# A transformer trunk on one core: the second part's down projection as four pairs in seven products, the third part's ninth gate/up unit ahead of it

## The chip, the core and the metric

The kernel runs on one core of a Trainium2 chip. The metric is the time of one execution on the device, in microseconds. The kernel before was run three times; its median is what the changed kernel is compared with.

## The reference, cut to what matters

Two layers, each with a feed-forward, a mixer (convolution and differential attention) and a second feed-forward, over 512 positions of 1024 channels in float32. The change lies in the feed-forwards, of which there are four:

```python
D_MODEL, SEQ, DEPTH, D_FF = 1024, 512, 2, 2816

def swiglu(h, w_gate, w_up, w_down):
    return (jax.nn.silu(h @ w_gate) * (h @ w_up)) @ w_down

for l in range(DEPTH):
    x = x + 0.5 * swiglu(rms_norm(x, ffn1_norm[l]), ffn1_w_gate[l], ffn1_w_up[l], ffn1_w_down[l])
    ...  # mixer
    x = x + 0.5 * swiglu(rms_norm(x, ffn2_norm[l]), ffn2_w_gate[l], ffn2_w_up[l], ffn2_w_down[l])
```

## The kernel before

**Number format.** Activations lie with channels on the 128 partitions and positions along the row. Every float32 product is made of three TensorE matmuls in the fp32r format: each operand is split into a high part (ScalarE copies it, `hi`, L364 for weights) and a low part (VectorE subtracts, `lo`, L368 for weights), and high x high, high x low and low x high are added up in PSUM.

**The three parts of a feed-forward.** The 2816 hidden channels are 22 tiles of 128. `PARTS` gives each part as (first tile, number of tiles, pairs): the first has five tiles and is computed plainly, the second eight tiles (5 to 12), the third nine (13 to 21). In the second and third parts the work is cut into units. A gate/up unit (`GateUp`) makes one hidden tile: its gate and its up projection together are a 2 x 2 block product (two outputs, two halves of the input channels, two halves of the positions), done in seven products of 256 columns instead of eight, after Strassen and Winograd. Each product has four steps over the input channels and three matmuls a step, so a unit is 84 matmuls of 256 columns. After the part's gate/up units come four down units (`Down`, q = 0 to 3), each for two output tiles, A = 2q and B = 2q + 1 of x. A down unit takes hidden tiles two by two: a pair of hidden tiles and two output tiles are again a 2 x 2 block, in seven products. Hidden tiles that are in no pair are multiplied plainly, with matmuls of 512 columns (`plain`; into the bank of its own for B, `ps_d`, it is called `spare`).

**What the units need.** For a weight unit, GpSimdE forms four sums of the weight quarters (`sums`, L355 to L358); then ScalarE and VectorE split four chunks A, B, C and D. For a pair of hidden tiles, the first tile is held as it is (`hold`), the second's difference is formed, and `combine` (L664 to L671) makes three sums, split into `hi`, `lo` and `four` (the tiles `hs`): `four` holds high and low part of the fourth sum, whose high part is L669 on ScalarE and whose low part is L671 on VectorE. `hi` and `lo` come from L668 and L670. The seven products name their operands: `t1`, `b11`, `b21`, `b22` read the split hidden tiles (`hh`, `hl`), and `t2`, `t3`, `t4` the sums.

**Order.** `Unit.body` runs one unit: product `t1`, then `t4`, then the rest of the unit before (`prev.rest()`, its product `t3`), then `b11`, `b21`, `b22`, `t2`, and `close`. In between it loads the next unit and splits its chunks in the order A, B, D, C, finishes the hidden tile of the unit before in three steps, and combines the pair of the unit two before. The first matmul of every product is pinned to its place in the program, so TensorE's order is that of `body`; the other engines' instructions are placed by the scheduler, once, when the program is built. Each engine then runs its list in order. The high parts of the 1024-wide chunks have four buffers in turn (`whi`), the raw chunks five (`wraw`), the D chunks one (`wraw2`). The copy L427 (`keep`, of the first bank after `t2`) must be over before `rest` of the same unit may start.

**The end of a feed-forward.** The last down unit (q = 3 of the third part) makes `spare` early, after `t4`; in `close` it makes the plain product for A, adds (L580), writes A into x (L571), subtracts and writes for B (L587, L571), and `rest` adds the last product into B. After each write `after` prepares the tile for the next stage, or, in the last feed-forward, sends it to the output.

Of the kernel before, what the change touches and what calls it, by code (L numbers as in the profile page):

```python
# [11 lines left out]
F32 = mybir.dt.float32  # L12
# [3 lines left out]
ALU = mybir.AluOpType  # L16
AX = mybir.AxisListType

P = 128
DEPTH = 2  # L20
SEQ = 512
DM = 1024
KT = DM // P
# [18 lines left out]
HS = SEQ // 2  # L42


PARTS = ((0, 5, 0), (5, 8, 3), (13, 9, 3))
PLAIN = PARTS[0][1]
PIN = False

# [20 lines left out]
def trunk(ctx: ExitStack, tc: tile.TileContext, xt, par, lamv, relb, onehot,  # L69
# [264 lines left out]
    def pinned(ins, pin=PIN):  # L334
        if pin:
            tc.keep_in_program_order(ins)
        return ins
# [4 lines left out]
    def by_two(t):  # L342
        return t.rearrange("p (n c) -> p n c", n=2)

    class Unit:
# [1 line left out]

        WIDE = {"A": ("", 1024), "B": ("", 1024), "C": ("", 1024), "D": ("2", 512)}

        def __init__(self, fp, turn):  # L350
            self.fp, self.turn = fp, turn
            self.parts, self.raw, self.cols = {}, {}, {}

        def sums(self, u1, u2, g1, g2, d, m0, m1):
# [36 lines left out]
        def body(self, nxt, prev, prev2):  # L391
            if nxt:
                nxt.load()
            self.begin()
            self.go(self.c, "u2u1", "t1", first=True)
            pinned(S.activation(self.keep[:, 3], self.c, AF.Copy))
            if nxt:
                nxt.hi("A")
                nxt.lo("A")
            self.go(self.d, "u2", "t4", first=True)  # L400
            self.early()
            if nxt and self.early_free:
# [24 lines left out]
            pinned(S.activation(self.keep[:, 2], self.a, AF.Copy))  # L427
# [7 lines left out]
        early_free = True  # L435

        def early(self):
            pass
# [4 lines left out]
        def finish(self, n):  # L443
            pass

        def extras(self):
            pass

    class GateUp(Unit):
        steps = KT // 2  # L450

        def __init__(self, fp, turn, halves, g, u, n, gated):
            super().__init__(fp, turn)
# [34 lines left out]
        def finish(self, n):  # L488
            self.gated.add(self.n, self.banks[0], n)

        def extras(self):
            self.gated.combine(self.n, self.banks[0])

    class Down(Unit):
        def __init__(self, fp, turn, dn, m0, many, pairs, q, h, after, last):
            super().__init__(fp, turn)
# [51 lines left out]
        def plain(self, ps, n, first=False):  # L548
            if 2 * self.steps == self.many:
                return  # L550
            w = [
                self.w("BA"[n], k) if k < 8 else self.w(*self.ninth[n])
                for k in range(2 * self.steps, self.many)
            ]
            self.product(ps, zip(w, self.h.hh[2 * self.steps :]), first)

        def spare(self):
            if 2 * self.steps < self.many:
# [41 lines left out]

    class Gated:

        def __init__(self, fp, pairs):
            self.fp, self.pairs = fp, pairs
            self.hh, self.sums, self.held, self.slots = [], [], {}, []

        def part(self):

# [12 lines left out]
        def plain(self, n, us):  # L621
            hi = self.fp.tile([P, SEQ], F32R, tag=f"hh{n}", name="hh")
            lo = self.fp.tile([P, SEQ], F32R, tag=f"hl{n}", name="hl")
            S.activation(hi, us, AF.Copy)
            V.tensor_tensor(lo, us, f32(hi), op=ALU.subtract)
            self.hh.append((hi, lo))

        def paired(self, n):
            return n < 2 * self.pairs
# [1 line left out]
        def add(self, n, us, step):  # L631
            a, b = slice(0, HS), slice(HS, SEQ)
            first = self.paired(n) and n % 2 == 0
            if step == 0:
                if first:
                    self.held[n] = self.fp.tile([P, SEQ], F32, tag=("hh8", "hl8")[n // 2 % 2], name="hold")
                    pinned(S.activation(self.held[n], us, AF.Copy))
                else:
                    self.part_hi(n, us)
            if step == 1:  # L640
                if first:
                    pinned(V.tensor_tensor(us[:, b], self.held[n][:, a], us[:, b], op=ALU.subtract))
                    self.part_hi(n, us)
                else:
                    self.part_lo(us)
            if step == 2 and first:
                self.part_lo(us)

        def part_hi(self, n, us):
            hi = self.fp.tile([P, SEQ], F32R, tag=f"hh{n}", name="hh")  # L650
            lo = self.fp.tile([P, SEQ], F32R, tag=f"hl{n}", name="hl")
            pinned(S.activation(hi, us, AF.Copy))
            self.hh.append((hi, lo))

        def part_lo(self, us):
            hi, lo = self.hh[-1]
            pinned(V.tensor_tensor(lo, us, f32(hi), op=ALU.subtract))

        def combine(self, n, us):
            if not self.paired(n) or n % 2 == 0:  # L660
                return
            a, b = slice(0, HS), slice(HS, SEQ)
            t = self.held[n - 1]
            pinned(V.tensor_tensor(t[:, b], us[:, b], t[:, b], op=ALU.subtract))  # L664
            pinned(V.scalar_tensor_tensor(t[:, a], t[:, a], -1.0, t[:, b], op0=ALU.mult, op1=ALU.subtract))
            pinned(V.scalar_tensor_tensor(us[:, a], us[:, a], -1.0, t[:, a], op0=ALU.mult, op1=ALU.subtract))
# [3 lines left out]
            pinned(V.tensor_tensor(lo, t, f32(hi), op=ALU.subtract))  # L670
            pinned(V.tensor_tensor(four[:, b], us[:, a], f32(four[:, a]), op=ALU.subtract))  # L671
            self.sums.append((hi, lo, four))
# [9 lines left out]
    def ffn(pr, gu, dn, after, turn, lead=None, aside=None):  # L682
        with tc.tile_pool(name="ffn", bufs=1) as fp:
            r = halves = None
            held, h = [], Gated(fp, 0)
            for m in range(PLAIN):
                if m == 4 and aside:
                    aside()
# [44 lines left out]
            units = []  # L733
            for m0, many, pairs in PARTS[1:]:
                h = Gated(fp, pairs)
# [392 lines left out]
    turn = 0  # L1128
# [91 lines left out]
```

## Time and profile before

| | |
|---|---|
| median of three runs | 1781.65 us (1780.59 to 1783.45) |
| profiled execution | 1779.9 us |
| its span | 1778.1 us |
| TensorE busy | 1765.5 us, 99% of the span |
| VectorE, ScalarE, GpSimdE busy | 78%, 56%, 54% |
| granted TensorE clock | 1.000 |

The span runs from the first to the last instruction; the profiled execution's own time is 1.8 us longer. Engines go by the names PE (TensorE's matmuls), PEld (its weight loads), DVE (VectorE), ACT (ScalarE), POOL (GpSimdE) and SP. A row of the timeline gives start in us, duration in us, engine, line, instruction, tiles, shape and count, and in brackets the idle time of the engine before it with what ended it. Matmul rows overlap: the time from start to start is what one costs.

### The profile page before, as it was taken

Reading aid. Unit: us, or ns where it says so; the run is one execution under the profiler, and the core shown is the slowest. Engines: PE = TensorE matmul, PEld = TensorE weight load, DVE = VectorE, ACT = ScalarE, POOL = GpSimd, SP = SyncE. Lnnn points to the kernel's source line nnn. Section 1 sums busy time; section 2 is a strip of 40 time slices with the busy share of each in tenths; the row PEclk is TensorE's granted clock in tenths of the full one; section 3 lists DMA queues with packets and bytes.
Section 4 is the critical chain, followed back from the end, with each engine's and each line's share of the span. In section 5 each row is a group of like instructions: output and inputs, shape, how many; then the busy total and the mean of one; then the engine's idle time right before and its main releaser. Section 6 shows DMA issues by size and latency. Waiting matters only on the chain.

```text
span 1778.1 us, 30234 instructions
## 1 busy us (share of the span) xinstructions
PE 1765.5 (99%) x11725; PEld 1617.3 (91%) x11725; DVE 1394.3 (78%) x1997; ACT 986.9 (56%) x1579; POOL 965.4 (54%) x665
## 2 busy tenths in 40 slices
PE   9999999999999999999999999999999999999999
PEld 7899999988788899999988999999877888999998
DVE  6978787868857978788767887877788588787875
ACT  6456565645844456466534664665558354564663
POOL 2276566379952156566303655653898433565661
PEclk9999999999999999999999999999999999999999
DMA  6233333423122223333332333334230232333332
GB/s 225 96 113 96 107 107 105 144 85 96 47 72 83 83 95 107 107 98 118 118 95 72 108 96 108 106 102 148 72 119 25 72 107 73 106 96 108 107 105 75
DMA packets 74225, 177.87 MB, mean 100 GB/s; under 512 B 8951, under 2 KB 30726, under 8 KB 74080
## 3 DMA queue, kind: packets, MB, share of 16 engines
q1 hardware_dynamic: 72480, 174.10, 31.1%
q8 instruction: 92, 1.51, 0.3%
q0 software_dynamic: 1312, 1.67, 0.3%
q14 instruction: 53, 0.43, 0.1%
q10 hardware_dynamic: 288, 0.16, 0.0%
HBM read 173.79 MB, written 3.42 MB: 100 GB/s over the span
## 4 chain that ended last, share of the span: by engine, by line
PE 89%; DVE 6%; issue 2%; POOL 2%; ACT 1%; DMA 0%; DVEq 0%; SPq 0%; ACTq 0%
PE ps_pair L378 48%; PE ps_pair L141 5%; PE ps_pair L142 5%; PE ps_pair L138 5%; PE ps_d L378 3%; DVE wlo L368 2%; PE ps_d L141 2%; PE ps_d L142 2%; PE ps_d L138 2%; PE ps_sc L990 2%; PE ps_pair L867 2%; PE ps_pair L868 2%; PE ps_pair L866 2%; PE ps_out L138 1%; PE ps_out L142 1%
## 5 line engine op out<-in xcount | busy, mean ns | idle before, releaser
L368 DVE TENSOR_TENSOR wlo<-wraw,whi 128x1024 fp32r<-128x1024 f32 (+4 forms) x400 | 510.3, 1277 | 171.9 <-ACT whi L364 171.4
L364 ACT ACTIVATE whi<-wraw 128x1024 fp32r<-128x1024 f32 (+4 forms) x400 | 373.6, 935 | 333.5 <-PE ps_pair L378 153.1
L355 POOL TENSOR_TENSOR wraw<-wraw 128x512 f32<-128x512 f32 (+1 forms) x100 | 127.8, 1278 | 554.7 <-DVE wlo L368 366.5
L378 PE MATMUL ps_pair<-acth,wlo 128*128 128x256 f32 x1088 | 307.9, 283 | 0.0
L378 PE MATMUL ps_pair<-actl,whi 128*128 128x256 f32 x1088 | 307.9, 283 | 0.0
L378 PE MATMUL ps_pair<-acth,whi 128*128 128x256 f32 x1088 | 307.9, 283 | 0.0
L378 PE MATMUL ps_pair<-th,whi 128*128 128x256 f32 x816 | 231.8, 284 | 1.2 <-ACT keep L427 0.4
L378 PE MATMUL ps_pair<-tl,whi 128*128 128x256 f32 x816 | 230.9, 283 | 0.0
L378 PE MATMUL ps_pair<-th,wlo 128*128 128x256 f32 x816 | 230.9, 283 | 0.0
L378 PEld LDWEIGHTS ps_pair<-actl,whi 128*128 128x128 f32 x1088 | 208.9, 192 | 0.2
L378 PEld LDWEIGHTS ps_pair<-acth,whi 128*128 128x128 f32 x1088 | 208.9, 192 | 0.2
L378 PEld LDWEIGHTS ps_pair<-acth,wlo 128*128 128x128 f32 x1088 | 208.9, 192 | 0.0
L101 ACT ACTIVATE whi<-wraw 128x1024 fp32r<-128x1024 f32 (+3 forms) x124 | 123.2, 1000 | 150.5 <-PE ps_pair L141 84.3
L141 PE MATMUL ps_pair<-actl,whi 128*128 128x512 f32 x448 | 174.6, 390 | 0.6 <-DVE actl L227 0.5
L142 PE MATMUL ps_pair<-acth,wlo 128*128 128x512 f32 x448 | 174.2, 390 | 0.0
L138 PE MATMUL ps_pair<-acth,whi 128*128 128x512 f32 x448 | 173.6, 393 | 0.1
L357 POOL TENSOR_TENSOR wraw<-wraw 128x512 f32<-128x512 f32 (+1 forms) x100 | 169.3, 1693 | 7.9
L358 POOL TENSOR_TENSOR wraw<-wraw 128x512 f32<-128x512 f32 (+1 forms) x100 | 164.3, 1643 | 7.8
L378 PEld LDWEIGHTS ps_pair<-th,whi 128*128 128x128 f32 x816 | 156.6, 192 | 3.1 <-ACT keep L427 3.1
L378 PEld LDWEIGHTS ps_pair<-th,wlo 128*128 128x128 f32 x816 | 156.6, 192 | 0.0
L378 PEld LDWEIGHTS ps_pair<-tl,whi 128*128 128x128 f32 x816 | 156.6, 192 | 0.0
L356 POOL TENSOR_TENSOR wraw<-wraw 128x512 f32<-128x512 f32 (+1 forms) x100 | 149.9, 1499 | 7.6
(203 smaller groups left out, 4402.1 us busy)
## 6 DMA issues: line engine op xcount, KB each, us to landing
wraw<-in_gu SPq DMA_DIRECT2D x172, 512.0 KB, 3.5
wraw<-in_wqkv SPq DMA_DIRECT2D x24, 512.0 KB, 3.5
wraw<-in_wag SPq DMA_DIRECT2D x16, 512.0 KB, 3.6
wraw<-in_wout SPq DMA_DIRECT2D x16, 512.0 KB, 3.5
wraw<-in_dn SPq DMA_DIRECT2D x60, 128.0 KB, 3.1
wraw<-in_dn SPq DMA_DIRECT2D x20, 384.0 KB, 3.2
wraw<-in_dn SPq DMA_DIRECT2D x28, 256.0 KB, 3.1
wraw<-in_dn SPq DMA_DIRECT2D x20, 320.0 KB, 3.5
```

The source lines that it names most:

```text
L101: S.activation(hi, raw, AF.Copy)
L138: first = T.matmul(ps, wh, xh, start=start, stop=False)
L141: T.matmul(ps, wh, xl, start=False, stop=False)
L142: T.matmul(ps, wl, xh, start=False, stop=stop)
L355: G.tensor_tensor(d, g1, u1, op=ALU.add)
L356: G.tensor_tensor(u1, u1, u2, op=ALU.add)
L357: G.tensor_tensor(m0, u1, g1, op=ALU.add)
L358: G.tensor_tensor(m1, m0, g2, op=ALU.add)
L364: pinned(S.activation(hi[:, : self.cols[k]], self.raw[k][:, : self.cols[k]], AF.Copy), pin)
L368: pinned(V.tensor_tensor(out=lo[:, :c], in0=self.raw[k][:, :c], in1=f32(hi[:, :c]), op=ALU.subtract), pin)
L378: mm = T.matmul(ps, l, r, start=first and i == n == 0, stop=False, skip_group_check=True)
L866: T.matmul(ps[n], xh[:, t], wh, start=k == 0, stop=False)
```

## The change

The second part gets four pairs instead of three, so its four down units have no plain products. The fourth pair, made of its seventh and eighth hidden tiles, can only be combined after its eighth gate/up unit. The third part's ninth gate/up unit (tile index 8) is placed between that one and the first down unit, and the fourth pair is combined right behind it (`soon`), at the end of the next unit's `body` instead of in the one after that. `hold` uses other buffers in the third part (`hh7`, `hl7`), as the ninth unit's hidden tile now lies in `hh8` and `hl8` from early on. The second part's first down unit now splits the next one's chunk B early, as the others do (`early_free`). The last down unit of a feed-forward makes `spare` in `close`, ahead of the plain product for A, which now follows the addition; the writes for B come ahead of the write for A.

```diff
-PARTS = ((0, 5, 0), (5, 8, 3), (13, 9, 3))
+PARTS = ((0, 5, 0), (5, 8, 4), (13, 9, 3))
...
@@ Unit.body
-            if prev2:
-                prev2.extras()
+            if prev2 and not prev2.soon:
+                prev2.combine()
             self.go(self.c, "all", "b22")
             self.go(self.a, "g1u2u1", "t2")
             pinned(S.activation(self.keep[:, 2], self.a, AF.Copy))
             self.close()
+            if prev and prev.soon:
+                prev.combine()
...
@@ GateUp.__init__
+            self.soon = n == 2 * gated.pairs - 1 and n + 1 == gated.many
...
@@ Down
-            self.early_free = q > 0
+            self.early_free = early_free
...
         def early(self):
-            if self.early_free:
+            if self.early_free and not self.last:
                 self.spare()
...
         def close(self):
             A, B = 2 * self.q, 2 * self.q + 1
             two, keep = by_two(self.banks[1]), self.keep
-            if not self.early_free or self.last:
+            late = not self.early_free or self.last
+            rest = 2 * self.steps < self.many
+            if self.last:
+                self.spare()
+            elif late:
                 self.plain(self.banks[1], 0)
             pinned(V.tensor_tensor(two, two, keep[:, 0::2], op=ALU.add))
-            self.into(A, two, 0.5)
-            self.after(A)
-            if not self.early_free:
+            if self.last:
+                self.plain(self.banks[1], 0)
+            else:
+                self.into(A, two, 0.5)
+                self.after(A)
+            if late and not self.last:
                 self.spare()
-            if 2 * self.steps < self.many:
-                two = by_two(self.ps)
-                pinned(V.tensor_tensor(two, two, keep[:, 1::2], op=ALU.subtract))
-                self.into(B, two, 0.5)
+            if rest:
+                pinned(V.tensor_tensor(by_two(self.ps), by_two(self.ps), keep[:, 1::2], op=ALU.subtract))
+                self.into(B, by_two(self.ps), 0.5)
+            if self.last:
+                self.into(A, two, 0.5)
+                self.after(A)
...
@@ Gated
-                    self.held[n] = self.fp.tile([P, SEQ], F32, tag=("hh8", "hl8")[n // 2 % 2], name="hold")
+                    self.held[n] = self.fp.tile([P, SEQ], F32, tag=self.hold[n // 2 % 2], name="hold")
...
@@ ffn
-                for n in range(many):
-                    units.append(GateUp(fp, turn, halves, gu[m0 + n, 0], gu[m0 + n, 1], n, h))
-                    turn += 1
+                gates = [
+                    GateUp(fp, halves, gu[m0 + n, 0], gu[m0 + n, 1], n, h)
+                    for n in (*range(8, many), *range(min(many, 8)))
+                ]
                 end = m0 + many == FT
-                for q in range(KT // 2):
-                    units.append(Down(fp, turn, dn, m0, many, pairs, q, h, after if end else lambda m: None,
-                                      end and q == KT // 2 - 1))
-                    turn += 1
+                units += gates[:1] + downs + gates[1:]
+                downs = [
+                    Down(fp, dn, m0, many, pairs, q, h, after if end else lambda m: None, q > 0 or not end,
+                         end and q == KT // 2 - 1)
+                    for q in range(KT // 2)
+                ]
+            units += downs
```

In the changed file the lines of `combine` are L677 to L684 instead of L664 to L671, the addition in `GateUp.close` is L481 instead of L478, and L364, L368, L378, L407 and L427 keep their numbers.

More of the change, by code (lines that the diff above doesn't have):

```diff
@@ L348, in trunk, with __init__ @@
         WIDE = {"A": ("", 1024), "B": ("", 1024), "C": ("", 1024), "D": ("2", 512)}
-        def __init__(self, fp, turn):
-            self.fp, self.turn = fp, turn
+        def __init__(self, fp):
+            self.fp = fp
             self.parts, self.raw, self.cols = {}, {}, {}
@@ L433, in body @@
                     nxt.lo("B")
-        early_free = True
+        early_free, soon = True, False
         def early(self):
@@ L489, in finish, with combine, __init__ @@
             self.gated.add(self.n, self.banks[0], n)
-        def extras(self):
+        def combine(self):
             self.gated.combine(self.n, self.banks[0])
     class Down(Unit):
-        def __init__(self, fp, turn, dn, m0, many, pairs, q, h, after, last):
-            super().__init__(fp, turn)
+        def __init__(self, fp, dn, m0, many, pairs, q, h, after, early_free, last):
+            super().__init__(fp)
             self.dn, self.m0, self.many, self.steps, self.q, self.h = dn, m0, many, pairs, q, h
             self.after, self.last = after, last
-            self.early_free = q > 0
+            self.early_free = early_free
         def load(self):
@@ L554, in plain @@
             ]
-            self.product(ps, zip(w, self.h.hh[2 * self.steps :]), first)
+            self.product(ps, zip(w, (self.h.hh[k] for k in range(2 * self.steps, self.many))), first)
         def spare(self):
@@ L601, in trunk, with __init__ @@
     class Gated:
-        def __init__(self, fp, pairs):
-            self.fp, self.pairs = fp, pairs
-            self.hh, self.sums, self.held, self.slots = [], [], {}, []
+        def __init__(self, fp, pairs, many):
+            self.fp, self.pairs, self.many = fp, pairs, many
+            self.hold = ("hh7", "hl7") if many > 8 else ("hh8", "hl8")
+            self.hh, self.sums, self.held, self.slots = {}, [], {}, []
         def part(self):
@@ L731, in ffn @@
             turn += KT // 2
-            units = []
+            units, downs = [], []
             for m0, many, pairs in PARTS[1:]:
-                h = Gated(fp, pairs)
-                for n in range(many):
-                    units.append(GateUp(fp, turn, halves, gu[m0 + n, 0], gu[m0 + n, 1], n, h))
-                    turn += 1
-                end = m0 + many == FT
-                for q in range(KT // 2):
-                    units.append(Down(fp, turn, dn, m0, many, pairs, q, h, after if end else lambda m: None,
-                                      end and q == KT // 2 - 1))
-                    turn += 1
+                h = Gated(fp, pairs, many)
+                gates = [
+                    GateUp(fp, halves, gu[m0 + n, 0], gu[m0 + n, 1], n, h)
+                    for n in (*range(8, many), *range(min(many, 8)))
+                ]
+                end = m0 + many == FT
+                units += gates[:1] + downs + gates[1:]
[5 more added lines that the diff above has]
+            units += downs
+            for unit in units:
+                unit.turn = turn
+                turn += 1
             units[0].load()
```

20 lines of the change are left out of this document (10 added, 10 removed).

## The prediction

> **What bounds the kernel now.** I read the page first, then the chain of waits, then the timeline engine by engine around the pair combinations.
>
> ```profile
> span 1778.1 us, 30234 instructions
> PE 1765.5 (99%) x11725; PEld 1617.3 (91%) x11725; DVE 1394.3 (78%) x1997; ACT 986.9 (56%) x1579; POOL 965.4 (54%) x665
> PEclk9999999999999999999999999999999999999999
> ```
>
> TensorE is busy for 1765.5 of 1778.1 us at full clock, so the other engines lie beneath it. Two things alone move the time: fewer matmul microseconds, and a place where TensorE, which runs its list in order, has to wait. The profiled execution took 1779.9 us, 1.8 more than its span; the median of the three runs, 1781.65, is 1.75 above that. I make the sum against the former and shift it to the latter.
>
> The chain gives the period of one down unit of the second part (its unpaired product, ps_d, comes once per unit). The ScalarE rows give that of a gate/up unit (the split of its third chunk, L364, is released by the same product in each unit).
>
> ```profile
> 182.84 1.39 PE ps_d L378 x6
> 193.16 1.39 PE ps_d L378 x6
> ...
> 146.96 1.06 ACT L364 ACTIVATE whi<-wraw 128x1024 fp32r<-128x1024 f32 x1 [0.78 <-PE ps_pair L378]
> ...
> 157.04 1.06 ACT L364 ACTIVATE whi<-wraw 128x1024 fp32r<-128x1024 f32 x1 [0.78 <-PE ps_pair L378]
> ```
>
> A down unit takes 193.16 - 182.84 = 10.32 us, a gate/up unit 157.04 - 146.96 = 10.08 us. The latter is 7 products x 4 pairs x 3 = 84 matmuls of 256 columns, so 0.120 us each. The former is 63 of those (7.56 us) and 12 of 512 columns, which leaves 2.76 us, 0.230 each.
>
> **Part by part: the seven products.** With four pairs a down unit of the second part is also 84 matmuls of 256 columns: 10.08 us, a saving of 0.24 us. There are 4 such units in each of 4 feed-forwards: 16 x 0.24 = 3.8 us off TensorE. (The built program has 336 matmuls of 256 columns more and 192 of 512 fewer, so the change does what it says.) As nine 512-column starts take 2.04 us (a row below), 0.227 each, the saving by starts alone is 12 x 0.227 - 21 x 0.120 = 0.20 per unit, 3.2 in all: that is the lower bound.
>
> [...]
>
> VectorE, ScalarE and GpSimdE gain work (chunks of 1024 and 512 columns instead of 768 and 384, sums of 512 instead of 384, one hold and one combination more per feed-forward), and per down unit VectorE gives up a write into x and a 512-wide subtraction for two 256-wide additions. Their cover is TensorE's 10.08 us per unit; it is gone where TensorE needs their result at once, and that is the next step.
>
> **The fourth pair's sums.** Before, three pairs are combined, the last of them (L664 to L671) while the eighth gate/up unit runs, a unit ahead of the first use. Now the fourth pair is made of the seventh and eighth units; only the third part's ninth unit lies between them and the first down unit. Its combination must give "four" (high part by ScalarE, low part by VectorE, the step of L671) for the second product of that down unit. Let T be the start of that unit on TensorE: twelve matmuls of the first product, nine for the other three pairs, one with the high part, so the low part is wanted at T + 22 x 0.120 = T + 2.64 us. When does it come? The built program's order on VectorE there is:
>
> ```
> L670 TensorTensor hl_1974<-ps_pair_1769,hh_1973 128x512
> L677 TensorTensor hold_1832<-ps_pair_1769,hold_1832 128x256
> L678 TensorScalarPtr hold_1832<-hold_1832 128x256
> L368 TensorTensor wlo_2066<-wraw_2035,whi_2065 128x1024
> L679 TensorScalarPtr ps_pair_1769<-ps_pair_1769,hold_1832 128x256
> L481 TensorTensor ps_pair_1911<-ps_pair_1911,keep_1912 128x512
> L683 TensorTensor hs_2028<-hold_1832,hs_2027 128x512
> L684 TensorTensor hs_2029<-ps_pair_1769,hs_2029 128x256
> ```
>
> Between the second and the third step stands a split of the second down unit's first chunk (L368). It is the order that the trace shows for every earlier combination, save that L671 moved ahead of the next split. In the third part, with the same widths as now (unit start first):
>
> ```profile
> 282.04 0.28 PE L378 MATMUL ps_pair<-acth,whi 128*128 128x256 f32 x1
> 282.17 1.06 ACT L364 ACTIVATE whi<-wraw 128x1024 fp32r<-128x1024 f32 x1 [1.32 <-POOL wraw L356]
> ...
> 282.93 0.41 DVE L664 TENSOR_TENSOR hold<-ps_pair,hold 128x256 f32<-128x256 f32 x1
> 283.37 0.48 DVE L665 SCALAR_TENSOR_TENSOR hold<-hold 128x256 f32<-128x256 f32 x1
> 283.77 2.32 DVE L368 TENSOR_TENSOR wlo<-wraw,whi 128x1024 fp32r<-128x1024 f32 x1
> 286.02 0.42 DVE L666 SCALAR_TENSOR_TENSOR ps_pair<-ps_pair,hold 128x256 f32<-128x256 f32 x1
> 286.35 0.68 DVE L478 TENSOR_TENSOR ps_pair<-ps_pair,keep 128x512 f32<-128x512 f32 x1
> 286.95 0.67 DVE L670 TENSOR_TENSOR hs<-hold,hs 128x512 fp32r<-128x512 f32 x1
> 287.55 1.21 DVE L368 TENSOR_TENSOR wlo<-wraw,whi 128x1024 fp32r<-128x1024 f32 x1
> 288.68 0.41 DVE L671 TENSOR_TENSOR hs<-ps_pair,hs 128x256 fp32r<-128x256 f32 x1
> ...
> 283.64 1.37 POOL L358 TENSOR_TENSOR wraw<-wraw 128x512 f32<-128x512 f32 x1
> ```
>
> With L671 at 287.55 its end is 287.96, T + 5.92; from the end of the split (286.09) to there are 1.87 us. The split took 2.32 us while a GpSimdE sum ran (283.64 to 285.01); the next one, with GpSimdE idle, 1.21. [...] Two other places bound it:
>
> ```profile
> 159.78 0.28 PE L378 MATMUL ps_pair<-acth,whi 128*128 128x256 f32 x1
> ...
> 161.00 1.95 DVE L368 TENSOR_TENSOR wlo<-wraw,whi 128x1024 fp32r<-128x1024 f32 x1
> ...
> 302.19 0.28 PE L378 MATMUL ps_pair<-hh,whi 128*128 128x256 f32 x1
> 302.32 1.06 ACT L364 ACTIVATE whi<-wraw 128x1024 fp32r<-128x1024 f32 x1 [1.44 <-issue]
> ...
> 303.42 1.22 DVE L368 TENSOR_TENSOR wlo<-wraw,whi 128x1024 fp32r<-128x1024 f32 x1 [1.29 <-ACT whi L364]
> ```
>
> At 159.78 the split ends at T + 3.17, so the low part comes at T + 5.04. At 302.19, with no sum beside it, the split ends at T + 2.45, so T + 4.32. Sooner I see no way: ScalarE's half of that split began 0.13 us after the unit's start in both rows, as its whi buffer (four in turn) is the one that the unit before read last. So TensorE waits for 5.92 - 2.64 = 3.3, 2.4 or 1.7 us. I take 2.8: the sums are 512 wide as at 282.04, but a sum need not fall on the split in full. Four times: 11.2 us (6.8 to 13.1).
>
> **The ninth unit ahead of it.** The eighth unit's last product waits for a copy (L427) that stands behind the split of the next chunk. Where the GpSimdE sums came late, it cost this:
>
> ```profile
> 131.94 0.28 PE L378 MATMUL ps_pair<-th,wlo 128*128 128x256 f32 x1
> 132.32 0.39 PE L378 MATMUL ps_pair<-th,whi 128*128 128x256 f32 x1
> ...
> 130.94 1.06 ACT L364 ACTIVATE whi<-wraw 128x1024 fp32r<-128x1024 f32 x1 [1.94 <-POOL wraw L356]
> 131.91 0.36 ACT L427 ACTIVATE keep<-ps_pair 128x256 f32<-128x256 f32 x1
> ...
> 128.75 2.16 POOL L356 TENSOR_TENSOR wraw<-wraw 128x512 f32<-128x512 f32 x1
> 290.10 1.02 POOL L355 TENSOR_TENSOR wraw<-wraw 128x384 f32<-128x384 f32 x1 [5.09 <-DVE wlo L368]
> 291.19 1.90 POOL L356 TENSOR_TENSOR wraw<-wraw 128x384 f32<-128x384 f32 x1
> ```
>
> That is a gap of 132.32 - 131.94 - 0.12 = 0.26, and 0.11 more behind it. The 384-wide sums at 290.10 ended at 293.09 and cost nothing in a unit that began at 282.04 + 10.08 = 292.12. At 512 wide they end some 0.5 us later (1.3 and 2.16 instead of 1.02 and 1.90), ScalarE is done with L427 at 293.6 + 1.33 = 294.96, and TensorE wants it at 292.12 + 2.88 = 295.00. It is just met or just missed: 0.2 us per feed-forward, 0.8 in all (0 to 1.5).
>
> What else moves costs nothing that I can see. The ninth unit's loads, sums and splits now stand ahead of four down units on the queues of SP, GpSimdE, ScalarE and VectorE, but whole units change places, each is still fetched one unit ahead, and TensorE's 10 us per unit cover it. The second down unit's second chunk is split earlier (early_free); its cover is the same. The waits such as that at 132.32 come behind a part's first combination, whose order stays, so I leave them in.
>
> **The last unit.** Its unpaired product for the last tile now runs ahead of the other one, so the subtraction and a write into x no longer queue behind TensorE's end:
>
> ```profile
> 312.34 2.04 PE ps_d L378 x9
> ...
> 1773.47 0.28 PE L378 MATMUL ps_pair<-hs,wlo 128*128 128x256 f32 x1
> 1773.52 1.29 DVE L571 SCALAR_TENSOR_TENSOR x<-ps_pair,x 128x512 f32<-128x512 f32 x2
> ```
>
> The last write now starts at 1773.52 + 0.60 = 1774.12; it could start as the last matmul ends, 1773.47 + 0.28, and a little: 0.3 us off, once (0 to 0.4). Where the feed-forward is not the last, TensorE goes on with the next stage and the change is hidden. The new wait in it (the unpaired product of tile 6 behind VectorE's addition) has 2.04 us of the other one as cover against some 1.2 of L427 and the addition.
>
> Sum: 1779.9 - 3.8 + 11.2 + 0.8 - 0.3 = 1787.8 us for a profiled execution, and 1781.65 + 7.9 = 1789.5 for the median.
>
> **The rivals.** *The wait stays hidden (faster).* If the split of the next chunk did not stand in the way, or the buffer came free earlier, the low part would be there by T + 2.64; then only -3.8 - 0.3 remains: 1777.5. For it: the first two steps are over by T + 1.8 at 282.04, and more of the unit before could be ahead. Against: it decides 1.7 us below the quickest of my three places. 8%.
>
> *The wait is half hidden.* If the low part comes at about T + 3.6, 1 us per feed-forward cancels the saving: about 1781.6. 5%.
>
> *The clock falls behind each wait.* At the start TensorE ran slow:
>
> ```profile
> 1.05 4.21 PE L162 MATMUL ps_idle<-ones_r 128*128 128x512 f32 x9 [1.05 <-DVE relb L759]
> ...
> 1327.28 0.50 PE L896 MATMUL ps_v<-whi,acth 128*128 128x512 f32 x1 [1.81 <-ACT qz L912]
> 1327.62 0.39 PE L897 MATMUL ps_v<-wlo,acth 128*128 128x512 f32 x1
> 1327.85 0.39 PE L898 MATMUL ps_v<-whi,actl 128*128 128x512 f32 x1
> ```
>
> Nine matmuls took 4.21 us there, 0.47 each, about half the pace. If each wait brought that back for as long, 4.2/2 = 2.1 us more in each feed-forward: 1789.5 + 8.4 = 1797.9. Against: after 1.81 us of idling the next came at 0.23. [...] 6%.
>
> **How the numbers follow.** The forecast has 81%, and by its bounds runs from 1781.65 - 3.8 + 6.8 - 0.4 = 1784.3 to 1781.65 - 3.2 + 13.1 + 1.5 = 1793.1; with half a microsecond for the spread of the runs the range is 1783.8 to 1793.6. A measurement of this kernel tells about 0.2% (3.6 us) from no change, so slower begins at 1785.2. Slower: 81% less 2% at its low end, and the clock's 6%: 0.85. Within: 5% and that 2%: 0.07. Faster: 0.08.
>
> **What the profile would show.** Right: four gaps of 2 to 3 us on TensorE, each in two pieces (for ScalarE's, then VectorE's part of hs), in the second product of the second part's first down unit; 10.08 us per down unit there; TensorE's busy time down by 3 to 4 us; nothing else over 0.4 us. Wrong: no such gaps, or L684 over before T + 2.64; down units that still take 10.3 us; or new gaps in the third part.

## The result and the profile after

The changed kernel takes 1793.39 us (median of six runs, 1791.0 to 1794.34). The kernel before took 1781.33 us in the six runs beside it (1780.59 to 1783.45). The ratio is 1.0064, 95% interval 1.0051 to 1.0077: slower by 12.1 us. The forecast was 1789.5 with a range to 1793.6, so the direction and most of the sum were right, and the time lies at the range's upper end. The 3.9 us between forecast and result are a second cause, which the prediction had named and thought unlikely.

The page of the profiled execution (1793.42 us) begins:

```profile
span 1791.6 us, 30559 instructions
PE 1770.4 (99%) x11869; PEld 1628.4 (91%) x11869; DVE 1414.6 (79%) x2021; ACT 998.7 (56%) x1591; POOL 991.9 (55%) x665
```

TensorE's busy time rose by 4.9 us although it has less work, and the page's row of the clock is as before, full tenths throughout: both are too coarse here. Only the mean granted clock of the whole span, 0.995 instead of 1.000, hints at more than a wait. The view of the waits, with columns total, times and longest in us, names the new stall (there is no row of hs on TensorE before):

```profile
PE ps_pair L378 <- ACT hs L682: 5.6, 4, 1.4
PE ps_pair L378 <- DVE hs L684: 3.5, 4, 0.9
```

Four waits for the high part and four for the low part, one pair in each feed-forward. The timeline of TensorE in the first feed-forward shows the shape, and something behind it:

```profile
182.54 0.28 PE L378 MATMUL ps_pair<-hs,wlo 128*128 128x256 f32 x1
184.21 0.38 PE L378 MATMUL ps_pair<-hs,whi 128*128 128x256 f32 x1 [1.39 <-ACT hs L682]
185.46 0.58 PE L378 MATMUL ps_pair<-hs,whi 128*128 128x256 f32 x1 [0.87 <-DVE hs L684]
...
186.06 0.41 PE L378 MATMUL ps_pair<-th,whi 128*128 128x256 f32 x1
186.27 0.41 PE L378 MATMUL ps_pair<-tl,whi 128*128 128x256 f32 x1
...
188.77 0.28 PE L378 MATMUL ps_pair<-hl,whi 128*128 128x256 f32 x1
188.89 0.28 PE L378 MATMUL ps_pair<-hh,wlo 128*128 128x256 f32 x1
```

Start to start less the matmul's own 0.12 us, the two gaps are 184.21 - 182.54 - 0.12 = 1.55 and 185.46 - 184.21 - 0.12 = 1.13 us; with the 0.1 lost on the matmul after them, 2.78 us. Behind them the matmuls start every 0.213 us instead of every 0.12; at 188.77 the full pace is back. In the fourth feed-forward the same two gaps are followed by full pace:

```profile
1617.67 0.28 PE L378 MATMUL ps_pair<-hs,wlo 128*128 128x256 f32 x1
1619.34 0.38 PE L378 MATMUL ps_pair<-hs,whi 128*128 128x256 f32 x1 [1.39 <-ACT hs L682]
1620.59 0.38 PE L378 MATMUL ps_pair<-hs,whi 128*128 128x256 f32 x1 [0.87 <-DVE hs L684]
...
1620.93 0.28 PE L378 MATMUL ps_pair<-th,whi 128*128 128x256 f32 x1
1621.05 0.28 PE L378 MATMUL ps_pair<-tl,whi 128*128 128x256 f32 x1
```

The view by stretches gives the granted clock. Its columns are the stretch, its length, the busy time and count of instructions of each engine, the clock, the DMA share and GB/s. A count is of all matmuls that touch a stretch. The stretches end where the clock changes, or would on the same grid:

```profile
181.85:185.27 3.42, 1.36 (x10) 0.95 (x8) 3.27 (x5) 2.17 (x6) 2.60 (x2) 1.00 0.18 65
185.27:188.68 3.41, 3.22 (x15) 3.22 (x16) 1.36 (x2) 1.09 (x2) 0.00 (x0) 0.50 0.00 0
727.99:731.40 3.41, 1.50 (x10) 1.30 (x11) 2.24 (x5) 1.67 (x3) 1.35 (x1) 1.00 0.00 0
731.40:734.81 3.41, 3.41 (x18) 3.41 (x18) 2.97 (x5) 1.00 (x2) 0.77 (x1) 0.50 0.21 63
1072.73:1076.15 3.42, 1.35 (x10) 0.95 (x8) 3.27 (x5) 2.16 (x6) 2.59 (x2) 1.00 0.16 58
1076.15:1079.56 3.41, 3.22 (x15) 3.23 (x16) 1.36 (x2) 1.10 (x2) 0.00 (x0) 0.50 0.00 0
1615.46:1618.87 3.41, 2.49 (x21) 2.28 (x20) 2.54 (x5) 2.12 (x4) 3.25 (x3) 1.00 0.48 154
1618.87:1622.28 3.41, 2.07 (x15) 1.88 (x16) 1.84 (x4) 2.04 (x3) 0.78 (x1) 1.00 0.02 5
1622.28:1625.70 3.42, 3.42 (x30) 3.42 (x30) 3.02 (x5) 1.55 (x3) 1.30 (x1) 1.00 0.37 114
```

After three of the four waits TensorE ran at half clock for 3.41 us. The starts lie whole multiples of 3.4133 us apart: 731.40 - 185.27 = 160 times, 1076.15 - 731.40 = 101 times. So they stand on a fixed grid, and four equal waits lie on it in different ways. Ten matmuls touch the 3.41 us ahead of each fall in the down units, of 30 in a stretch without a wait (the last row); the fourth wait is cut by an edge 1.1 us after its first gap begins, with 21 matmuls in the one stretch and 15 in the other, and no fall came. The stretches ahead of the three falls were not idle: they held 1.36, 1.50 and 1.35 us of busy time.

The first down unit of the second part took 14.25, 14.35, 14.27 and 12.85 us in the four feed-forwards, so the half pace cost 1.40 to 1.50 us each over the undisturbed fourth, 4.3 in all. Two more falls stand in the mixers, at 499.29 and 1338.97 (92 and 338 grid steps from the first). The second is the place that the prediction quoted at 1327.28:

```profile
1338.21 0.50 PE L916 MATMUL ps_v<-whi,acth 128*128 128x512 f32 x1 [1.80 <-ACT qz L932]
...
1339.06 0.63 PE L916 MATMUL ps_v<-whi,acth 128*128 128x512 f32 x1
1339.48 0.63 PE L917 MATMUL ps_v<-wlo,acth 128*128 128x512 f32 x1
```

The idling is the same as before (1.80 us), but now the matmuls behind it start every 0.42 us instead of 0.23. The two lengthened the mixers by 0.7 and 1.6 us.

The down units answer as forecast (rows of ScalarE's third split, released by the same product in each unit):

```profile
201.76 1.06 ACT L364 ACTIVATE whi<-wraw 128x1024 fp32r<-128x1024 f32 x1 [0.81 <-PE ps_pair L378]
...
211.84 1.06 ACT L364 ACTIVATE whi<-wraw 128x1024 fp32r<-128x1024 f32 x1 [0.80 <-PE ps_pair L378]
```

211.84 - 201.76 = 10.08 us. The span of 1791.6 is then 1778.1 + 11.1 (waits) + 4.3 and 2.3 (half clock) + 0.6 (the ninth unit) - 3.8 (work) - 0.4 (the end) - 0.6 (a stall of the kernel before at 1575.73 that did not come again) + 0.1 at the start = 1791.7.

### The profile page after: what moved, and what is told of

Same layout as the page of the kernel before. It is cut to its first block, busy times and chain, and to the rows that moved or that the text cites. A ratio compares the mean times of both kernels' runs of the same rounds, so it can differ in the third digit from the quotient of the medians.

```text
span 1791.6 us, 30559 instructions
## 1 busy us (share of the span) xinstructions
PE 1770.4 (99%) x11869; PEld 1628.4 (91%) x11869; DVE 1414.6 (79%) x2021; ACT 998.7 (56%) x1591; POOL 991.9 (55%) x665
## 3 DMA queue, kind: packets, MB, share of 16 engines
q8 instruction: 93, 1.52, 0.3%
## 5 line engine op out<-in xcount | busy, mean ns | idle before, releaser
L368 DVE TENSOR_TENSOR wlo<-wraw,whi 128x1024 fp32r<-128x1024 f32 (+2 forms) x400 | 521.9, 1305 | 169.5 <-ACT whi L364 168.9
L364 ACT ACTIVATE whi<-wraw 128x1024 fp32r<-128x1024 f32 (+2 forms) x400 | 378.7, 948 | 328.6 <-PE ps_pair L378 160.8
L355 POOL TENSOR_TENSOR wraw<-wraw 128x512 f32<-128x512 f32 (+1 forms) x100 | 128.2, 1282 | 538.2 <-DVE wlo L368 362.5
L378 PE MATMUL ps_pair<-acth,wlo 128*128 128x256 f32 x1088 | 307.9, 283 | 0.0
L378 PE MATMUL ps_pair<-actl,whi 128*128 128x256 f32 x1088 | 307.9, 283 | 0.0
L378 PE MATMUL ps_pair<-acth,whi 128*128 128x256 f32 x1088 | 307.9, 283 | 0.0
L378 PE MATMUL ps_pair<-th,whi 128*128 128x256 f32 x816 | 233.4, 286 | 0.9
L378 PE MATMUL ps_pair<-tl,whi 128*128 128x256 f32 x816 | 232.2, 285 | 0.0
L378 PE MATMUL ps_pair<-th,wlo 128*128 128x256 f32 x816 | 232.2, 285 | 0.0
L378 PEld LDWEIGHTS ps_pair<-actl,whi 128*128 128x128 f32 x1088 | 208.9, 192 | 0.2
L378 PEld LDWEIGHTS ps_pair<-acth,whi 128*128 128x128 f32 x1088 | 208.9, 192 | 0.2
L378 PEld LDWEIGHTS ps_pair<-acth,wlo 128*128 128x128 f32 x1088 | 208.9, 192 | 0.0
L358 POOL TENSOR_TENSOR wraw<-wraw 128x512 f32<-128x512 f32 (+1 forms) x100 | 174.4, 1744 | 7.8
L357 POOL TENSOR_TENSOR wraw<-wraw 128x512 f32<-128x512 f32 (+1 forms) x100 | 173.4, 1734 | 7.8
L356 POOL TENSOR_TENSOR wraw<-wraw 128x512 f32<-128x512 f32 (+1 forms) x100 | 161.9, 1619 | 7.6
L378 PEld LDWEIGHTS ps_pair<-th,whi 128*128 128x128 f32 x816 | 157.8, 193 | 2.9 <-ACT keep L427 2.5
L378 PEld LDWEIGHTS ps_pair<-th,wlo 128*128 128x128 f32 x816 | 157.9, 194 | 0.0
L378 PEld LDWEIGHTS ps_pair<-tl,whi 128*128 128x128 f32 x816 | 157.9, 193 | 0.0
```

Of the source, the lines that this page charges most:

```text
L355: G.tensor_tensor(d, g1, u1, op=ALU.add)
L356: G.tensor_tensor(u1, u1, u2, op=ALU.add)
L357: G.tensor_tensor(m0, u1, g1, op=ALU.add)
L358: G.tensor_tensor(m1, m0, g2, op=ALU.add)
L364: pinned(S.activation(hi[:, : self.cols[k]], self.raw[k][:, : self.cols[k]], AF.Copy), pin)
L368: pinned(V.tensor_tensor(out=lo[:, :c], in0=self.raw[k][:, :c], in1=f32(hi[:, :c]), op=ALU.subtract), pin)
```

## The experiments

Four things were asked above all. Does the wait and nothing else cost the 11 us? Does the half clock come from it, and is it worth 4.3? Is the order on VectorE, as the prediction said, what makes the low part late? And do the seven products gain anything once it is hidden?

**Keep TensorE at work while it waits.** Twelve matmuls whose results are read by nothing stand in the first down unit's second product, ahead of the fourth pair's part:

```diff
+FILL = 12
...
-            self.go(self.d, "u2", "t4", first=True)
+            if prev2 and prev2.soon:
+                todo = [(self.weights("u2", j), self.feats("t4", j)) for j in range(self.steps)]
+                self.product(self.d, todo[:3], True)
+                ps = bank("tp", "ps_fill")
+                for n in range(FILL):
+                    tc.keep_in_program_order(
+                        T.matmul(ps, ones_r, ones_r.unsqueeze(1).broadcast_to([P, NT, P]), start=True, stop=True))
+                self.product(self.d, todo[3:])
+            else:
+                self.go(self.d, "u2", "t4", first=True)
```

> The changed kernel, with twelve matmuls of 512 columns that nothing reads put in front of the fourth pair's part of the second product of the second part's first down unit (2.7 us of TensorE's time, about the wait there). Theory (the clock is halved behind three of the four waits because TensorE idles, 1.5 us each): the fill takes the place of the wait, no half-speed stretch follows in those units, so 1793.4 - 4.4 = about 1789.0 us. Rival A (the matmuls behind the wait are slow for another reason, late operands say): unchanged, 1793.4 us. Rival B (there is no wait to fill, the time is spent elsewhere): slower by the fill, 4 x 2.7 us, 1804 us.

Measured: 1788.34 us (1787.04 to 1790.38), ratio to the kernel before 1.0043 [1.003, 1.0057]. TensorE's timeline:

```profile
182.77 2.91 PE L407 MATMUL ps_fill<-ones_r 128*128 128x512 f32 x12
185.52 0.48 PE L379 MATMUL ps_pair<-hs,whi 128*128 128x256 f32 x2
...
185.95 0.28 PE L379 MATMUL ps_pair<-th,whi 128*128 128x256 f32 x1
186.07 0.28 PE L379 MATMUL ps_pair<-tl,whi 128*128 128x256 f32 x1
```

The fourth pair starts at 185.52, as late as with the wait, and all behind it runs at full pace (0.12 us from start to start), in all four feed-forwards. The first down unit takes 12.87 to 12.89 us everywhere, close to the 12.85 of the changed kernel's undisturbed fourth one. Work that does nothing made the kernel 5 us faster than the changed one.

**Less filling.** The same with five matmuls, which leave part of the wait idle: a test of how much idling it takes.

```diff
-FILL = 12
+FILL = 5
```

> The changed kernel with five matmuls of 512 columns whose results are read by nothing (5 x 0.227 = 1.13 us) in front of the fourth pair's part of the first down unit's second product, in place of the twelve of the earlier run. They lie within the wait of 2.78 us and leave some 1.6 us of it idle. My theory, by which the half-pace stretches come only from a 3.41 us window that TensorE spends mostly idle (0.67 and more, while 0.50 was followed by none): every first down unit takes 10.08 + 2.78 = 12.86 us as in the undisturbed fourth one of the changed kernel, none has a half-pace stretch, and the time is that of the changed kernel less 4.3 us, 1789.1 (1787.5 to 1790.5). Rival, by which any wait of over a microsecond brings the slow stretch: three or four units of 14.3 us, 1793.4.

Measured: 1787.43 us (1786.29 to 1789.11), 1.0032 [1.0021, 1.0044]: 0.07 us under my range and far from the rival's 1793.4. Two idle pieces are left, and no half pace follows:

```profile
182.87 1.31 PE L407 MATMUL ps_fill<-ones_r 128*128 128x512 f32 x5
184.42 0.39 PE L379 MATMUL ps_pair<-hs,whi 128*128 128x256 f32 x1 [0.24 <-ACT hs L692]
185.69 0.39 PE L379 MATMUL ps_pair<-hs,whi 128*128 128x256 f32 x1 [0.88 <-DVE hs L694]
...
186.03 0.28 PE L379 MATMUL ps_pair<-th,whi 128*128 128x256 f32 x1
```

The stretches of the grid that hold the waits of the first three feed-forwards stand at full clock, and so do those behind them:

```profile
183.13:186.54 3.41, 2.28 (x13) 1.57 (x12) 2.50 (x5) 1.51 (x4) 1.61 (x1) 1.00 0.00 0
725.85:729.26 3.41, 2.29 (x12) 1.54 (x11) 2.90 (x5) 1.53 (x5) 2.01 (x1) 1.00 0.03 9
1070.60:1074.01 3.41, 2.28 (x13) 1.53 (x12) 2.73 (x5) 1.51 (x5) 1.84 (x1) 1.00 0.01 2
```

So around these waits, stretches with 1.35 to 1.50 us of busy time were followed by half clock (three times), and those with 2.07 to 2.29 were not (four times). One more row narrows the gap: near the end of the changed kernel's last down unit a stretch with 1.53 us (1786.12 to 1789.53) was followed by full clock (1.00 to the end of the span). So in the down units the two outcomes lie as close as 1.50 and 1.53 us of busy time. The wait is worth 11 us, the half clock behind it some 4 to 5.

**Combine sooner.** The combination moves up from the end of the ninth unit's `body` to the place ahead of its product `b21`, and its neighbours are held back: `close` and the low part of the next unit's third chunk until the combination's low part, and, in the unit after, the high part of the next first chunk until the combination's high part. (`behind(unit, n)` orders what it encloses after the high part, n = 0, or the low part, n = 1, of that unit's combination.)

```diff
@@ Unit.body
-                nxt.hi("A")
+                with behind(prev2, 0):
+                    nxt.hi("A")
...
             if prev:
                 prev.finish(2)
+            if prev and prev.soon:
+                prev.combine()
             self.go(self.b, "g2", "b21")
             self.middle()
...
             self.go(self.a, "g1u2u1", "t2")
             pinned(S.activation(self.keep[:, 2], self.a, AF.Copy))
-            self.close()
-            if prev and prev.soon:
-                prev.combine()
+            with behind(prev, 1):
+                self.close()
+                if nxt:
+                    nxt.lo("C")
             if nxt:
-                nxt.lo("C")
...
```

> The changed kernel, with the fourth pair's combination issued ahead of the neighbouring splits: VectorE's close of the ninth unit and the low part of chunk C come behind its low part, ScalarE's high part of the second down unit's chunk A behind its high part. No work is added or left out. Theory (wait 4 x 2.8 us for the fourth sum, and 4.4 us of half clock behind it): both gone, 1793.4 - 11.1 - 4.4 = about 1778 us, which is less than the kernel before by the saving of TensorE's matmuls. Rival (the splits that now come later are wanted just as soon): the wait moves to the first or second down unit and most of it stays, 1786 to 1793 us.

Measured: 1780.84 us (1779.22 to 1783.98), 0.9998 [0.9989, 1.0007]. That is 12.5 us faster than the changed kernel and no different from the kernel before: between my 1778 and the rival's 1786 to 1793. The first down unit still takes 11.03 us; 0.96 of the 2.78 stayed, in each of the four feed-forwards. The timelines of TensorE, VectorE and GpSimdE say why:

```profile
183.65 0.38 PE L381 MATMUL ps_pair<-hs,whi 128*128 128x256 f32 x1 [0.72 <-DVE hs L690]
...
180.03 1.52 DVE L684 SCALAR_TENSOR_TENSOR hold<-hold 128x256 f32<-128x256 f32 x1
181.59 0.43 DVE L685 SCALAR_TENSOR_TENSOR ps_pair<-ps_pair,hold 128x256 f32<-128x256 f32 x1
...
183.18 0.41 DVE L690 TENSOR_TENSOR hs<-ps_pair,hs 128x256 fp32r<-128x256 f32 x1
...
179.98 1.29 POOL L360 TENSOR_TENSOR wraw<-wraw 128x512 f32<-128x512 f32 x1
```

L684, which reads two tensors from SBUF, took 1.52 us instead of 0.47 to 0.48 (24 of its 28 counterparts, L678, in the changed kernel's profile): GpSimdE's sum had begun 0.05 us ahead of it, and L684 ended 0.28 us after that sum did. L685, which reads PSUM and SBUF, took 0.43 us although the next sum ran beside it (181.35 to 182.71); its counterpart L679 took 0.42 in the changed kernel, with a sum beside it and without. L689, which also reads two tensors from SBUF, began under that next sum and took 1.01 us (182.25 to 183.26) instead of the 0.67 of its counterpart L683 with no sum beside it. These two delays, 1.04 and 0.34 us on VectorE's way to L690, are enough for the 0.96 us that stayed of the wait; no run takes the sums out of the way, so this is worked out and not tried.

**The order alone.** The changed kernel with three pairs in the second part: the ninth unit ahead and the last unit reordered, but no fourth pair.

```diff
-PARTS = ((0, 5, 0), (5, 8, 4), (13, 9, 3))
+PARTS = ((0, 5, 0), (5, 8, 3), (13, 9, 3))
```

> The changed kernel with three pairs in the second part as before, so that only the order of the units, the hold buffers and the last unit differ from the kernel before. Theory (the loss is the wait for the fourth pair, the order costs nothing): 1781.3 - 0.4 (end) = about 1781 us. Rival (the ninth unit ahead of the down units costs by itself, through the loads and splits of a unit in another place): 3 to 12 us slower than before.

Measured: 1780.21 us (1779.09 to 1783.18), 0.9994 [0.9985, 1.0003]. TensorE has no new wait: within the interval, all of the loss hangs on the fourth pair.

**The ninth unit's last product first.** In the first down unit, twelve matmuls that must run anyway go ahead of the second product.

```diff
+            late = prev2 and prev2.soon
+            if late:
+                prev.rest()
             self.go(self.d, "u2", "t4", first=True)
             ...
-            if prev:
+            if prev and not late:
                 prev.rest()
```

> The changed kernel, with the ninth unit's last product (12 matmuls, 1.44 us) ahead of the second product in the first down unit, so that the fourth sum is wanted 1.44 us later. Theory (wait 2.8 us, and the clock falls only behind a window in which TensorE idles for some two thirds): wait 1.3 us, no fall in those units: 1793.4 - 5.8 - 4.4 = about 1783 us. Rival (the clock falls behind any wait of over a microsecond): 1793.4 - 5.8 = 1787.6 us.

Measured: 1784.18 us (1782.32 to 1784.78), 1.0013 [1.0004, 1.0022]: 9.2 us faster than the changed kernel, near my 1783, and its profile has no half clock (mean granted clock 1.000). The first down unit takes 11.76 us. The 1.44 us of matmuls cover only 1.1 of the 2.78, as the product moved forward has a wait of its own, for its copy `keep`:

```profile
PE ps_pair L378 <- DVE hs L687: 2.5, 4, 0.6
PE ps_pair L378 <- ACT keep L430: 2.2, 4, 0.6
```

**Both.** What the early combination left (0.96) is less than 1.44.

> The changed kernel with both remedies: the fourth pair's combination brought forward, and the ninth unit's last product placed ahead of the first down unit's second product. My theory: the wait that the early combination left (0.98 us in each first down unit) is shorter than the twelve matmuls that now lie in front of it (12 x 0.120 = 1.44 us), so no wait of TensorE for hs is left, all four first down units take 10.1 us, the eighth gate/up unit 10.2, no half-pace stretch stands in them, and the seven products show for the first time: 1780.84 - 4 x 0.98 = 1776.9 us, faster than the kernel before by some 4 us (1776 to 1778.5). Rival: the early combination moves the waits elsewhere (ScalarE's and VectorE's splits come late by what the combination takes), and a wait stays: 1779 to 1781.

Measured: 1778.38 us (1776.77 to 1780.21), 0.998 [0.9971, 0.9989]. This is the first version that is faster than the kernel before, by 3.4 us, and the time lies in my range of 1776 to 1778.5. The first down unit takes 10.08 us everywhere; but the rival had a point too, for the third down unit takes 10.16, 10.26, 10.92 and 10.14. Its worst case, in the third feed-forward:

```profile
1088.32 0.50 PE L381 MATMUL ps_pair<-hs,whi 128*128 128x256 f32 x2 [0.59 <-ACT keep L436]
...
1086.93 1.06 ACT L367 ACTIVATE whi<-wraw 128x1024 fp32r<-128x1024 f32 x1 [3.90 <-POOL wraw L359]
1087.90 0.37 ACT L436 ACTIVATE keep<-ps_pair 128x256 f32<-128x256 f32 x1
...
1084.74 2.16 POOL L359 TENSOR_TENSOR wraw<-wraw 128x512 f32<-128x512 f32 x1
```

The copy L436 stands behind a split that waited for a GpSimdE sum of 2.16 us. The four third units lose 1.2 us together (0.08 + 0.18 + 0.84 + 0.06). Against the kernel before, 1776.9 meant 1776.9 - 1781.0 = -4.1 us, and -3.4 was measured, so these waits are enough for what is missing, which is less than the interval.

**The last unit's order undone**, in the kernel with both:

```diff
-            if self.early_free and not self.last:
+            if self.early_free:
                 self.spare()
...
-            if self.last:
-                self.spare()
-            elif late:
+            if late:
                 self.plain(self.banks[1], 0)
             pinned(V.tensor_tensor(two, two, keep[:, 0::2], op=ALU.add))
-            if self.last:
-                self.plain(self.banks[1], 0)
-            else:
-                self.into(A, two, 0.5)
-                self.after(A)
+            self.into(A, two, 0.5)
+            self.after(A)
...
-            if self.last:
-                self.into(A, two, 0.5)
-                self.after(A)
```

> As the kernel with both remedies, with the reorder of a feed-forward's last unit undone. My theory: only the end of the program shows it, where the last matmul stands 4.65 us before the end of the span instead of 4.2: 0.4 us longer, 1777.3 us. Rival: the reorder makes the first three feed-forwards' hand-over to the next stage later or earlier as well, and the difference is over 1 us either way.

Measured: 1779.43 us (1777.49 to 1780.01), 0.9986 [0.9977, 0.9995]. The medians lie 1.05 us apart, more than the 0.4 expected and about what the rival asked for, but the runs of one and the other overlap. The profiles decide, by their last microseconds; the whole spans do not, as the mean granted clock was 0.998 in the kernel with both and 0.999 in the other. Spans and last writes into x, the kernel with both first:

```profile
span 1777.5 us, 30554 instructions
1773.56 0.69 DVE L583 SCALAR_TENSOR_TENSOR x<-ps_pair,x 128x512 f32<-128x512 f32 x1 [0.38 <-PE ps_pair L381]
```

```profile
span 1777.1 us, 30556 instructions
1772.52 1.29 DVE L583 SCALAR_TENSOR_TENSOR x<-ps_pair,x 128x512 f32<-128x512 f32 x2
```

The spans are 1777.48 and 1777.11 to the hundredth. With the reorder the last matmul starts at 1773.24, 4.24 us ahead of the end; without it at 1772.47, 4.64. It is worth 0.4 us, once, and the hand-over from the second to the third feed-forward did not change (from start to start 341.98 and 341.93 us).

## Why the prediction was right, and where it was short

**The seven products**: -3.8 forecast, 16 x (10.32 - 10.08) = -3.8 found, from 0.120 us a matmul of 256 columns and 0.230 of 512.

**The fourth pair's sums**: 2.8 each forecast, 2.78 found in every feed-forward, in two pieces and at the instruction named. The cause is the order on VectorE, as the prediction read it from the built program:

```profile
182.00 1.40 DVE L368 TENSOR_TENSOR wlo<-wraw,whi 128x1024 fp32r<-128x1024 f32 x1 [0.84 <-ACT whi L364]
183.32 0.42 DVE L679 SCALAR_TENSOR_TENSOR ps_pair<-ps_pair,hold 128x256 f32<-128x256 f32 x1
...
185.00 0.41 DVE L684 TENSOR_TENSOR hs<-ps_pair,hs 128x256 fp32r<-128x256 f32 x1
```

The split L368 stands ahead of L679, and VectorE even idles 0.84 us for it. The unit began at T = 180.15; the split ended at T + 3.25 and L684 at T + 5.26, both between the places that the prediction went by, while TensorE wanted the low part at T + 2.64. In the kernel that takes the splits off this path the wait fell by 1.8 of the 2.78 us, which shows that the order is the cause; what share falls to the split L368 alone was not tried, as `close` (L481) moved behind the combination with it. That the value matched to 0.02 us is partly luck, since it was chosen between 1.7 and 3.3.

**The ninth unit ahead**: 0.2 each forecast, 0.15 found (its successor's start is 10.23 instead of 10.08 us later), behind the copy named. **The last unit**: -0.3 forecast, -0.4 found, and -0.4 by the experiment that undoes it.

**The step that failed is the clock.** The prediction gave 6% to half pace behind each wait, priced at 2.1 us each. It came behind three of four, at 1.4 to 1.5, and cost 4.3 us, with some more in the mixers. The 6% was my estimate: in the profile before, whose mean granted clock is 1.000, no wait after the start has half pace behind it. The argument against it was a row: after 1.81 us of idling the next matmul came at 0.23. That row shows one execution and one position on the grid; the same idling (1.80 us) was followed by half pace, 0.42 us from start to start, in the changed kernel's profile. That a matmul breaks the wait did not keep the fall off either: the waits of 2.78 us, each broken by one matmul, were followed by half clock three times of four. The length to set the waits against is the 3.41 us of the grid that the changed kernel's profile shows: with two gaps of 1.55 and 1.13 us nearly end to end, one stretch is more than half idle unless an edge cuts the wait well inside, as in the fourth feed-forward. Without half clock in the down units the forecast's sum comes near what was measured: +7.9 us against the kernel before forecast, +5.6 and +7.3 in the kernels with five and with twelve filling matmuls, whose first down units take just as long.

That 1793.4 still lies within the range is luck. The range's top of 1793.6 was made for longer waits (13.1 us) and a dearer ninth unit (1.5), neither of which came; the half clock, which filled that room, was left out of it.

Two signs of being right that the prediction named did not appear. Nothing else was to cost over 0.4 us, and the half clock cost 1.4 to 1.5 three times. And TensorE's busy time, to be down by 3 to 4 us, rose by 4.9: half-pace matmuls count as busy (18 of them fill the 3.41 us from 731.40 on; 30 fill a stretch at full clock). Even in the kernel with the last product first, whose profile has no half clock, it fell by 2.1 us only (1763.4), so that sign was badly chosen.

The same terms give the other kernels. Each is the extra time of the first down units (in the kernel with both, of the third ones), plus 0.6 for the ninth unit, less 4.2 (3.8 for the seven products and 0.4 for the last unit). Half clock in the mixers is left out; runs of the kernel before have some half clock too (their mean granted clock is 0.997 to 1.000):

| kernel | worked out, us | measured against before, us |
|---|---|---|
| changed | 11.1 + 4.3 + 0.6 - 4.2 = +11.8 | +12.1 |
| filled with twelve, with five | 11.1 + 0.6 - 4.2 = +7.5 | +7.3, +5.6 |
| last product first | 6.7 + 0.6 - 4.2 = +3.1 | +3.2 |
| combined sooner | 3.8 + 0.6 - 4.2 = +0.2 | -0.2 |
| both | 1.2 (third unit) + 0.6 - 4.2 = -2.4 | -3.4 |

The intervals are about 2 us either way, so the differences under that are not told apart.

## What to carry to other kernels

A stage that saves work is paid for where its first result is wanted: write down when the last operand is ready and when TensorE asks for it, in the built order of each engine, before counting the matmuls saved (here 3.8 us saved against 11.1). A wait of TensorE can cost more than its length, since half clock may follow (here behind 2.78 us three times of four); put work that must run anyway into it, and here even matmuls whose results nothing reads were better than none. One row of idling without half clock behind it is weak evidence: here four equal waits lay on the grid in different ways, and one of them had no half clock behind it.

## What the runs showed that I had not expected

- **Half clock after stretches that are not idle.** In the down units, stretches of 3.41 us with 1.35 to 1.50 us of TensorE's busy time were followed by half clock, those with 1.53, 2.07 and more were not. In the mixers busy time does not part the cases: a stretch with 1.98 us was followed by half clock in the kernel with five filling matmuls (493.74 to 497.16), and one with 1.95 us by full clock in the kernel before (1323.52 to 1326.93). What exactly is counted stays open.
- **Half clock in the first mixer without the change's waits.** Besides the changed kernel (499.29 to 502.70), the kernel with five filling matmuls has it there, at 0.50 from 497.16 to 500.57, and so has the one with the last unit's order undone, from 496.64 to 500.06, which has no wait for the fourth pair. So the changed kernel's fall there (0.7 us) need not come from the change's waits. In the second mixer the profile before has full clock at that place of the program (1.00 from 1326.93 to 1330.35); what brought the changed kernel's fall there (1.6 us) stays open.
- **The spread of the runs follows the clock.** Of the 27 runs of the kernel before beside the first experiments, those with a granted clock of 1.000 took 1779.7 to 1780.1 us and those with 0.998 or 0.997 took 1782.5 to 1783.5. One stretch of 3.41 us at half clock lowers the mean by 0.5 x 3.41 / 1780 = 0.001, so by this estimate the latter had two or three of them. The changed kernel's 0.995 and 0.996 are four to five; its profile shows five.
- **Behind the start of a GpSimdE sum, a VectorE instruction with two SBUF inputs took 1.28 to 1.52 us instead of 0.47**, also where it is on the path of TensorE: 1.52 us in the kernel that combines sooner (L684, 0.05 us behind), and 1.28 to 1.29 in four places of the changed kernel's profile (L678, 0.01 us behind), each ending 0.28 us after the sum. In the other 24 places of that profile L678 began 0.23 to 0.28 us ahead of a sum and took 0.47 to 0.48. How close it may come is not told: four of the kernel before (L665) began within 0.005 us of a sum's start, on either side, and took 0.43.
